# Three Strassen steps in each branch unit, operands laid at any offset, a held preparation, one load moved, and halves, in a hybrid decoder block

## The chip, the cores and the metric

The kernel runs on one core of one Trainium2 chip. The metric is the device time of one execution, in microseconds (us). The profile is of one further execution. In it PE is TensorE's matrix multiplication, PEld its loading of the stationary operand, DVE is VectorE, ACT is ScalarE, POOL is GpSimd, and SP is SyncE, which issues the loads of the weights.

## The reference

One layer of a decoder block on x of 256 rows and 4096 columns, in float32:

```python
h = rmsnorm(x, norm_w)
u_p, z_p, u_c, b_c, c_c, z_c, g_logit = split(h @ w_in)          # 4096 x 20480
y_pool = causal_multiscale_pool(u_p, pool_w, pool_scale) * silu(z_p)
y_conv = causal_gated_shortconv(u_c, b_c, c_c, conv_w, conv_b) * silu(z_c)
br     = [y_pool @ w_branch[0], y_conv @ w_branch[1]]            # 2048 x 4096 each
merged = sum over n of sigmoid(g_logit[n] + gate_b[n]) * br[n]
out    = rmsnorm(x + merged @ w_out, final_norm_w)               # 4096 x 4096
```

## The kernel before

**Products.** Every float32 operand is split into a rounded high part and the remaining low part, and each block product is made of three matmuls: high by high, high by low, low by high. A column of work is a *unit* of 1024 output columns: four for the convolution path twice over (`cz`, `cb`, `cu`, `cc`), two for each half of the pooling path (`pz`, `pu`), eight gate units `g0_0` to `g1_3`, eight branch units `b0_0, b1_0, b0_1, ... b1_3`, and four output units `o0` to `o3`. They run in this order.

**Steps.** A unit is a string of steps, one for each 256 rows of its weight matrix, and the strings at the head of the file (L34 to L48) say which kind each step is. A `P` step is plain: 8 groups of 3 matmuls, 24 in all, into four PSUM banks E (`sums`). An `S` step uses Strassen's scheme with seven block products: 7 groups, 21 matmuls, into three of the banks E and the four banks F (`shared`). The price of an S step is more preparation on the other engines. A branch unit has eight steps.

**Preparation.** A step's weights (1 MB) are loaded by SP into one of three buffers `raw`. For a P step ACT rounds them into four cells of a ring of 15 cells (`highs`), and DVE forms the rest (`lows`). For an S step ACT rounds three cells, DVE forms sums of the quarters in the tile `parts` together with the lows of these three cells (`added`), and then ACT rounds the four sums into four more cells and DVE forms their lows (`split`). `pump` (L964) sends these pieces out in the order of the steps, as far ahead as a limit and free cells allow; it is called after each group of matmuls (`after_group`, L1008), when the cells that this group used have been released. Each engine works through its instructions in the order in which they were sent out.

**Ends of units.** When a bank has had its last matmul, `after_group` at once sends out a copy by ACT: of an E bank into the tile E (or Y), of an F bank into the unit's `join` slot (the tile Y for a gate unit, `last_pair` for a branch unit, E or a `raw` buffer elsewhere). With the last F bank DVE forms the corner sums there, and `combine` (L412) adds them to E. A P step closes its four E banks with its last four groups. An S step at a unit's end takes its products in an order of its own (L340), which closes E with its first three groups; the fourth E bank gets nothing from an S step. What remains to be done for the unit, its epilogue, is a list of items of which one is taken at each *tick*, that is after every 6 matmuls (L998).

**Operands.** The stationary operands (x, then the branches' y, then the merged m) stand in one buffer `arena` of 82 pieces of 1 KB a partition: eight regions of 4 for P, six of 7 and one of 8 for S; a last S region of 8 lies in `last_pair`. `y_ops` (L480) says where the operands of the two branches lie: 6 P and 2 S for branch 0, 5 P and 3 S for branch 1, where one S region of 8 also serves as a P operand in `b1_3`. During `g1_3` and the first branch units these are filled from DRAM through two staging tiles `sa` and `sb`: a load on POOL's queue, eight ticks for landing, then (for S) four sums by DVE, a copy by ACT and the lows by DVE (`Fill`, L751, `pop_fill`, L782). A fill waits until all operands that lay there before have been used. The operands for `o0` are filled in the same way from `b0_3` on.

**The gates.** The epilogue of a gate unit (L671) adds the bias by two accumulating loads on POOL's queue, applies the sigmoid on ACT and stores the result to DRAM (`gates_d`). For the last one, `g1_3`, the gate of branch 0, column 0 is then loaded into Y, on POOL's queue, for `b0_0`'s epilogue, which multiplies with it. The other gates are loaded in the epilogues of the branch units.

Of the kernel before, what the change touches and what calls it, by code (L numbers as in the profile page):

```python
# [15 lines left out]
P = 128  # L16
# [7 lines left out]
KB = 256  # L24
# [18 lines left out]
NINE_B = "PSPSPSPSSPSSPSPS"  # L43
HOST = "PPPBPPMMPSPSSPSSPSS"
OUT3 = "PSPSPSPSPSPSSPPP"
B0 = "PPPPSPSP"
B1 = "PSPSPSPP"
B1_LAST = "PSPPSPPP"  # L48


@with_exitstack
def hybrid_block(ctx: ExitStack, tc: tile.TileContext, x, xc, prm, rows_in, w_in, pool_w, w_branch, w_out, out):
# [101 lines left out]
    def place(region):  # L154
        kind, i = region
        if kind == "p":
            return 4 * KB * i, 4
        if kind == "q":
            return (4 * ND + 14 + 4 * i) * KB, 4
        if i < NS:  # L160
            return (4 * ND + 7 * i) * KB, 7
        return (4 * ND + 7 * NS + 8 * (i - NS)) * KB, 8
# [57 lines left out]
    def highs(cells, src):  # L220
        for i, c in runs(cells):
            act(ring[:, c, 0], src[:, i])
# [14 lines left out]
    class Step:  # L237
        def __init__(self, unit, kind, src=None, op=None, **kw):
            self.unit, self.kind, self.src, self.op = unit, kind, src, op
            self.__dict__.update(kw)  # L240
            self.raw = None
            self.prepared = False
            self.pre, self.mid = [], []

        def first(self):
            if self.kind == "B":
                return []

            def rounded(cells):
                self.q = self.raw.rearrange("p (i c) -> p i c", i=4)  # L250
                self.cells = cells
                if self in steps[:2]:
                    for i in range(4):
                        if self is steps[0] and i == 0:
                            copy(ring[:, cells[0], 0], self.q[:, 0])
                        else:
                            highs(cells[i:i + 1], self.q[:, i:i + 1])
                else:
                    highs(cells, self.q[:, 0:len(cells)])

            return [(3 if self.kind == "S" else 4, None, rounded)]

        def rest(self):
            if self.kind == "P":
                def rests(_):
                    if self in steps[:2]:
                        for i in range(4):
                            if self is steps[0] and i % 2 == 0:
                                x_low(0, 1 - i // 2)
                            lows(self.cells[i:i + 1], self.q[:, i:i + 1])  # L270
                    else:
                        lows(self.cells, self.q)

                return [(None, None, rests)] + self.mid
            if self.kind == "S":
                def added(_):
                    q = self.q
                    add(sums[:, 0:2], q[:, 3:4].to_broadcast([P, 2, NH]), q[:, 1:3])
                    lows(self.cells[2:3], q[:, 2:3])
                    add(sums[:, 2], sums[:, 0], q[:, 2])  # L280
                    lows(self.cells[0:2], q[:, 0:2])
                    add(sums[:, 3], sums[:, 2], q[:, 0])

                def split(cells):
                    self.sum_cells = cells
                    highs(cells[0:2], sums[:, 0:2])
                    for i in (2, 3):
                        highs(cells[i:i + 1], sums[:, i:i + 1])
                    lows(cells[0:2], sums[:, 0:2])
                    lows(cells[2:4], sums[:, 2:4])  # L290

                return [(None, None, added)] + self.mid + [(4, None, split)]
            if self.kind == "B":
                def parts(cells):
                    self.cells = cells
                    highs(cells, quarters(E))
                    lows(cells, quarters(E))

                return [(4, lambda: self.unit.flags.get("base"), parts)]

            def pooled(cells):
                self.pool_cells = cells
                q = quarters(E)[:, 2 * self.g:2 * self.g + 2]
                highs(cells, q)
                lows(cells, q)

            return [(None, None, lambda _: lows(self.cells, self.q)),
                    (2, lambda: self.unit.flags.get(f"pooled{self.g}"), pooled)]
# [160 lines left out]
    def gap(n):  # L469
        return [None] * n  # L470
# [5 lines left out]
    def make_ops(kinds):  # L476
        return [Operand(k, r) for k, r in kinds]

    x_ops = make_ops([("P" if r[0] == "p" else "S", r) for r in x_regions])
    y_ops = [make_ops([("P", ("p", i)) for i in range(6)] + [("S", ("s", i)) for i in (0, 1)]),  # L480
             make_ops([("P", r) for r in (("p", 6), ("p", 7), ("q", 0), ("q", 1), ("q", 2))] +
                      [("S", ("s", i)) for i in (6, 4, 5)])]
    m_ops = make_ops([("P" if r[0] == "p" else "S", r) for r in x_regions])

    def sequence(text, np_, total, both):
# [185 lines left out]
    def gate_unit(n, c):  # L671
        def epi(u):
            def bias(t):
                gather(E[:, t], gate_b[n, None, c * NU:(c + 1) * NU].to_broadcast([P, NU]))

            pause = side_items() + gap(3) if (n, c) == (0, 0) else gap(12)
            return (rescale(E) if u.late else gap(1)) + [lambda: bias(0), lambda: bias(1)] + pause + [
                lambda: act(E[:, 0], E[:, 0], AF.Sigmoid), None,
                lambda: act(E[:, 1], E[:, 1], AF.Sigmoid), lambda: move(gates_d[n, c], E)] + (
                    [lambda: move(Y, gates_d[0, 0])] if (n, c) == (1, 3) else [])  # L680
        text = HOST if (n, c) == (0, 0) else SEVEN3 if (n, c) == (1, 3) else NINE
        u = in_unit(f"g{n}_{c}", 6 * HALF + n * D + c * NU, epi, text)
        u.rotates, u.late = False, (n, c) != (1, 3)
# [4 lines left out]
    def branch_unit(n, c):  # L688
        def epi(u):
            if n == 0:  # L690
                return gap(8) + [lambda: mul(Y, E, Y)]
            turned = spare() if c < 3 else Y

            def gated():
                mul(E, E, spare())
                if c == 3:
                    last_pair["stack"].close()
                    open_last(F32R)
                    last_pair["again"] = True

            def copy(j):
                act(chan(turned)[:, 2 * j:2 * j + 2], bankview(j))

            def stored():
                put(m_d[c], chan(turned))
                merged[c] = now[0] + STORED
            return [lambda: move(spare(), gates_d[1, c])] + gap(6) + [gated, lambda: add(E, E, Y), None,
                lambda: c < 3 and move(Y, gates_d[0, c + 1])] + gap(3) + pairs(transposes(E, copy)) + [stored]

        text = (B1_LAST if c == 3 else B1) if n else B0  # L710
        u = Unit(f"b{n}_{c}", lambda i: w_branch[n, c, i], seq_y(text), y_ops[n], epi)
        u.urgent, u.lead, u.rotates = (lambda: None), 3, False
        units.append(u)
# [104 lines left out]
    insert(names["g0_0"], 1, names["pu1"])  # L818

    steps = [s for u in units for s in u.steps]  # L820
    last = units[-1]
    assert all(s.kind == "P" for s in last.steps[-TAIL:])
    tail = last.steps[-TAIL:]
# [181 lines left out]
            rg.release(part)  # L1005
        state["mm"] += len(mm)

    def after_group(u, b, st):  # L1008
        if u is not last:
            if b in u.total and u.closed([b]) and b not in u.flags:  # L1010
                u.flags[b] = True
                if b[0] == "E":
                    evacuate(u, b[1], b[2])
                else:
                    u.pending.append(b)
        if u.s and u is not last:
            corner_sums(u)
        while state["mm"] >= TICK:
            state["mm"] -= TICK
            tick()  # L1020
        state["limit"] = state["now"] + min(AHEAD, state["now"] + 1)
        if u.urgent and st is u.steps[-1]:
            state["limit"] = state["now"] + u.lead
        pump()

    fetch_x(0)
    act(ssq[:, 0, 0:1], ident[:, 0:1])
    pump()

    def room(o):  # L1030
        return range(o.o, o.o + (4 if o.region[0] in "pq" else 7 if o.region[1] < NS else 8) * KB, KB)

    holders = {c: o for o in x_ops for c in room(o)}
    for ops in (y_ops[0], y_ops[1], m_ops):
# [17 lines left out]
    def run_step(u, st):  # L1052
        if st.kind in "BM":
            (band_sums if st.kind == "B" else mix)(st)
            state["mm"] += 10 if st.kind == "B" else 24
            after_group(u, None, st)
            return
        while not st.op.ready:
            pop_fill(st.op)
        gs = st.groups()  # L1060
        for i, g in enumerate(gs):
            multiply(u, st, g)
            if i == len(gs) - 1:
                st.op.left -= 1
            after_group(u, g[0], st)

    def open_side():
        stack = ExitStack()
# [138 lines left out]
```

## Time and profile before

| | |
|---|---|
| median of 3 runs | 2381.3 us (2380.99 to 2381.68) |
| profiled execution | 2383.08 us, span 2381.4 us |
| granted TensorE clock in it, mean | 0.998 |
| ACT, POOL busy | 63%, 5% |
| data moved | 560.23 MB, 235 GB/s |
| a weight load of 1 MB, median from issue to landing | 4.9 us (w_in), 5.0 us (w_branch, w_out) |

The span runs from the first to the last instruction; the execution's own time is a little longer. A row of the groups or of the timeline gives the line of the code, the engine, the operation, what it writes and reads, its shape and the count, then its time; in square brackets stands how long the engine had been idle before it and what ended that. As nearly every instruction is recorded in a helper, many rows carry the helper's line: L59 is any ACT instruction, L62 a DVE operation on two tensors, L1002 a matmul of a step.

### The profile page before, as it was taken

What the parts mean: (1) busy time and instruction counts of PE and PEld (TensorE: products, weight loads), DVE (VectorE), ACT (ScalarE), POOL (GpSimd) and SP (SyncE); (2) the same over time, 40 slices, a digit from 0 to 9 for tenths busy, and PEclk for the clock granted to TensorE, in tenths of its full rate; (3) what the DMA queues carried; (4) which work ended last, traced back from release to release, by engine and by line L of the source; (5) the groups of instructions that cost most, each with busy time, mean ns of one, the idle gap of its engine ahead of it and who ended that gap; (6) DMA issues with size and microseconds to landing.
All of it is one profiled execution on the core that took longest, in us unless ns stands there. A gap on an engine that the chain in (4) does not pass through costs nothing.

```text
span 2381.4 us, 27763 instructions
## 1 busy us (share of the span) xinstructions
PE 2362.0 (99%) x10481; PEld 1950.3 (82%) x10481; DVE 2153.9 (90%) x2187; ACT 1502.4 (63%) x1626; POOL 113.4 (5%) x173
## 2 busy tenths in 40 slices
PE   9999999999999999999999999999999999999998
PEld 7888888888888888888888888888878888888886
DVE  8889989989989969969999999998998799899998
ACT  6665656666656556656666766666665566566664
POOL 0000000000001000100000000001100000000000
PEclk9999999999999999999999999999999999999999
DMA  9656646656657546746877787778766766767767
GB/s 347 224 196 231 227 171 252 231 204 226 224 180 260 215 176 215 241 176 217 267 250 245 248 249 243 230 255 270 267 252 234 255 231 244 252 210 256 256 218 268
DMA packets 90230, 560.23 MB, mean 235 GB/s; under 512 B 9968, under 2 KB 10224, under 8 KB 29168
## 3 DMA queue, kind: packets, MB, share of 16 engines
q1 hardware_dynamic: 69824, 485.39, 56.4%
q0 software_dynamic: 19696, 71.84, 11.5%
q8 instruction: 82, 1.34, 0.2%
q10 hardware_dynamic: 576, 1.24, 0.1%
q14 instruction: 52, 0.43, 0.1%
HBM read 519.63 MB, written 26.21 MB: 229 GB/s over the span
## 4 chain that ended last, share of the span: by engine, by line
PE 94%; DMA 2%; DVE 2%; ACT 1%; issue 1%; POOL 0%; SPq 0%; DVEq 0%; ACTq 0%; POOLq 0%
PE sums L1002 70%; PE shared L1002 22%; PE shared L656 1%; DMA raw<-in_w_in_dram 1%; PE shared L450 1%; DMA raw<-in_w_branch_dram 1%; ACT ring L59 1%; DVE ring L62 0%; DVE E L62 0%; DVE parts L62 0%; DMA sa<-y_d 0%; DVE raw L62 0%; DVE E L74 0%; ACT E L59 0%; ACT raw L59 0%
## 5 line engine op out<-in xcount | busy, mean ns | idle before, releaser
L1002 PE MATMUL sums<-ring,arena 128*128 128x512 f32 x7305 | 1707.6, 390 | 6.7 <-ACT E L59 3.1
L1002 PEld LDWEIGHTS sums<-ring,arena 128*128 128x128 f32 x7305 | 1371.1, 188 | 294.1 <-ACT E L59 3.5
L62 DVE TENSOR_TENSOR ring<-raw,ring 128x512 fp32r<-128x512 f32 (+3 forms) x720 | 963.2, 1345 | 161.9 <-ACT ring L59 157.1
L59 ACT ACTIVATE ring<-raw 128x1536 fp32r<-128x1536 f32 (+3 forms) x527 | 785.0, 1504 | 282.6 <-PE sums L1002 129.6
L59 ACT ACTIVATE ring<-parts 128x512 fp32r<-128x512 f32 (+1 forms) x621 | 465.6, 763 | 478.7 <-DVE parts L62 409.8
L1002 PE MATMUL shared<-ring,arena 128*128 128x512 f32 x2154 | 518.6, 389 | 0.0
L62 DVE TENSOR_TENSOR ring<-parts,ring 128x1024 fp32r<-128x1024 f32 (+1 forms) x430 | 480.1, 1161 | 7.7 <-ACT ring L59 7.5
L1002 PEld LDWEIGHTS shared<-ring,arena 128*128 128x128 f32 x2154 | 404.3, 188 | 84.1
L62 DVE TENSOR_TENSOR parts<-parts,raw 128x512 f32<-128x512 f32 x406 | 279.4, 688 | 0.0
L62 DVE TENSOR_TENSOR parts<-raw 128x1024 f32<-128x1024 f32 x203 | 247.6, 1220 | 7.7 <-DMA raw<-in_w_in_dram 6.3
L1002 PE MATMUL sums<-ring,last_pair 128*128 128x512 f32 x336 | 84.3, 396 | 0.0
L1002 PEld LDWEIGHTS sums<-ring,last_pair 128*128 128x128 f32 x336 | 63.2, 188 | 15.2
L1002 PE MATMUL shared<-ring,last_pair 128*128 128x512 f32 x192 | 47.6, 397 | 0.0
L59 ACT ACTIVATE E<-sums 128x512 f32<-128x512 f32 x72 | 41.5, 597 | 8.6 <-PE sums L1002 5.2
L1002 PEld LDWEIGHTS shared<-ring,last_pair 128*128 128x128 f32 x192 | 36.1, 188 | 8.7
L62 DVE TENSOR_TENSOR raw<-raw 128x512 f32<-128x512 f32 (+1 forms) x27 | 23.5, 870 | 9.7 <-ACT raw L59 8.8
L59 ACT ACTIVATE E<-sums,rin 128x512 f32<-128x512 f32 x28 | 17.6, 687 | 22.6 <-PE sums L1002 22.6
L62 DVE TENSOR_TENSOR E<-E,last_pair 128x2048 f32<-128x2048 f32 x12 | 27.5, 2289 | 3.3 <-ACT E L59 3.3
L59 ACT ACTIVATE last_pair<-shared 128x512 f32<-128x512 f32 x44 | 24.1, 597 | 9.4 <-PE shared L450 7.7
L62 DVE TENSOR_TENSOR E<-E,Y 128x2048 f32<-128x2048 f32 x13 | 29.7, 2287 | 0.1
L86 POOL DMA_DIRECT2D E<-Y x14 | 16.9, 1449 | 256.1 <-DVE Y L62 200.5
L59 ACT ACTIVATE Y<-shared 128x512 f32<-128x512 f32 x44 | 23.9, 603 | 4.4 <-PE shared L450 4.0
(132 smaller groups left out, 701.2 us busy)
## 6 DMA issues: line engine op xcount, KB each, us to landing
raw<-in_w_in_dram SPq DMA_DIRECT2D x318, 1024.0 KB, 4.9
raw<-in_w_branch_dram SPq DMA_DIRECT2D x64, 1024.0 KB, 5.0
raw<-in_w_out_dram SPq DMA_DIRECT2D x64, 1024.0 KB, 5.0
E<-in_rows_dram POOLq DMA_DIRECT2D x16, 512.0 KB, 6.8
gates_d<-E POOLq DMA_DIRECT2D x8, 1024.0 KB, 6.5
E<-Y POOLq DMA_DIRECT2D x14, 512.0 KB, 8.2
Y<-E POOLq DMA_DIRECT2D x10, 512.0 KB, 8.2
y_d<-E POOLq DMA_DIRECT2D x8, 512.0 KB, 6.7
```

Of the source, the lines that this page charges most:

```text
L59: return pin(nc.scalar.activation(dst, src, func, **kw))
L62: return pin(nc.vector.tensor_tensor(out=dst, in0=a, in1=b, op=op))
L86: return pin(nc.gpsimd.dma_start(dst, src, accum_op=ALU.add))
L450: pin(nc.tensor.transpose(shared(j)[:, i * T + t * P:i * T + (t + 1) * P], src[:, t, c:c + P], ident))
L656: pin(nc.tensor.matmul(o, a, b, start=(k, i) == (0, 0), stop=(k, i) == (3, 2)))
L1002: pin(nc.tensor.matmul(ps, lhs, rhs, start=n == 0, stop=n == u.total[b] - 1))
```

## The change

1. The operands of the branches may lie at any offset of the arena: a region of kind `y` gives its offset and its length. Both branches now have 5 P and 3 S operands, in 41 pieces each.
2. The string of the units `b0_c` becomes `PPPPSSPS` (three S steps in place of two, and an S step at the end), and `b1_3` gets the same string as the other `b1_c`, with three S steps in place of two.
3. During a unit's last step, if it is a P step, `pump` isn't called after the groups 3 to 6.
4. The load of the first gate is moved forward within the epilogue of `g1_3`, from behind the store of its result to the middle of the pause ahead of the sigmoids.
5. A P step that follows an S step is prepared in two halves: `highs` and `lows` each work on two cells at a time in place of four.

```diff
-B0 = "PPPPSPSP"
+B0 = "PPPPSSPS"
 B1 = "PSPSPSPP"
-B1_LAST = "PSPPSPPP"
...
-        if kind == "q":
-            return (4 * ND + 14 + 4 * i) * KB, 4
+        if kind == "y":
+            return i[0] * KB, i[1]
...
+                elif self.halved:
+                    for i in (0, 2):
+                        highs(cells[i:i + 2], self.q[:, i:i + 2])
                 else:
                     highs(cells, self.q[:, 0:len(cells)])
...
+                    elif self.halved:
+                        for i in (0, 2):
+                            lows(self.cells[i:i + 2], self.q[:, i:i + 2])
                     else:
                         lows(self.cells, self.q)
...
-    y_ops = [make_ops([("P", ("p", i)) for i in range(6)] + [("S", ("s", i)) for i in (0, 1)]),
-             make_ops([("P", r) for r in (("p", 6), ("p", 7), ("q", 0), ("q", 1), ("q", 2))] +
-                      [("S", ("s", i)) for i in (6, 4, 5)])]
+    y_ops = [make_ops([("P", ("y", (41 * n + 4 * i, 4))) for i in range(5)] +
+                      [("S", ("y", (i, 7))) for i in ((61, 68, 75) if n else (34, 20, 27))]) for n in range(2)]
...
             pause = side_items() + gap(3) if (n, c) == (0, 0) else gap(12)
+            if (n, c) == (1, 3):
+                pause = gap(5) + [lambda: move(Y, gates_d[0, 0])] + gap(6)
             return (rescale(E) if u.late else gap(1)) + [lambda: bias(0), lambda: bias(1)] + pause + [
                 lambda: act(E[:, 0], E[:, 0], AF.Sigmoid), None,
-                lambda: act(E[:, 1], E[:, 1], AF.Sigmoid), lambda: move(gates_d[n, c], E)] + (
-                    [lambda: move(Y, gates_d[0, 0])] if (n, c) == (1, 3) else [])
+                lambda: act(E[:, 1], E[:, 1], AF.Sigmoid), lambda: move(gates_d[n, c], E)]
...
-        text = (B1_LAST if c == 3 else B1) if n else B0
+        text = B1 if n else B0
...
     steps = [s for u in units for s in u.steps]
+    for a, b in zip(steps, steps[1:]):
+        b.halved = a.kind == "S" and b.kind == "P"
...
-    def after_group(u, b, st):
+    def after_group(u, b, st, hold=False):
...
-        pump()
+        if not hold:
+            pump()
...
-            after_group(u, g[0], st)
+            after_group(u, g[0], st, st is u.steps[-1] and st.kind == "P" and 3 <= i < len(gs) - 1)
```

More of the change, by code (lines that the diff above doesn't have):

```diff
@@ L241, in __init__ @@
             self.raw = None
-            self.prepared = False
+            self.prepared = self.halved = False
             self.pre, self.mid = [], []
@@ L1030, in room @@
     def room(o):
-        return range(o.o, o.o + (4 if o.region[0] in "pq" else 7 if o.region[1] < NS else 8) * KB, KB)
+        return range(o.o, o.o + place(o.region)[1] * KB, KB)
     holders = {c: o for o in x_ops for c in room(o)}
```

## The prediction

> **What bounds the kernel now.** I read the page first, then a piece of the chain of waits, then what PE (TensorE's matmuls) waits for, then the stages that the change touches. Times are us from the span's start.
>
> ```profile
> span 2381.4 us, 27763 instructions
> PE 2362.0 (99%) x10481; PEld 1950.3 (82%) x10481; DVE 2153.9 (90%) x2187; ACT 1502.4 (63%) x1626; POOL 113.4 (5%) x173
> 105.76 7.48 PE sums L1002 x33
> PE sums L1002 <- ACT E L59: 3.1, 1, 3.1
> PE sums L1002 <- ACT Y L59: 2.5, 2, 1.5
> ...
> PE sums L1002 <- DVE ring L743: 0.6, 1, 0.6
> PE sums L1002 <- DVE ring L62: 0.5, 1, 0.5
> ```
>
> PE sets the end: it is busy for 99% of the span. The third row, a piece of the chain of waits, prices a product: 7.48 / 33 = 0.2267 us. The other rows are nearly all that PE waits for: one wait for copies into E, two for copies into Y, and hardly any for DVE. So a gain comes from fewer products, or from these 5.6 us and what follows them; and DVE, at 90%, is close behind. The branch units, by stage:
>
> ```profile
> 1693.30:1738.80 45.50, 42.41 (x188) 34.79 (x187) 39.95 (x45) 29.64 (x34) 5.46 (x9) 1.00 0.83 283
> 1738.80:1782.00 43.20, 43.20 (x184) 35.59 (x185) 42.16 (x38) 27.49 (x29) 0.65 (x2) 0.96 0.58 210
> 1782.00:1825.90 43.90, 43.90 (x203) 36.53 (x202) 34.67 (x30) 24.42 (x28) 3.67 (x6) 1.00 0.75 273
> 1825.90:1867.40 41.50, 41.50 (x184) 34.37 (x184) 38.38 (x29) 25.56 (x25) 0.00 (x0) 1.00 0.60 216
> 1952.90:1996.90 44.00, 44.00 (x204) 36.59 (x203) 38.59 (x37) 27.53 (x36) 5.28 (x9) 1.00 0.79 284
> 1996.90:2039.00 42.10, 42.10 (x187) 34.89 (x186) 40.63 (x43) 27.68 (x30) 2.69 (x5) 1.00 0.67 240
> 1695.80:1770.10 74.30, 71.21 (x307) 58.47 (x307) 70.14 (x74) 45.88 (x51) 6.11 (x10) 0.98 0.70 244
> ```
>
> The rows are units b0_0, b1_0, b0_1, b1_1, b0_3 and b1_3, and a stretch over the first two; after the length stand PE, PEld, DVE, ACT and POOL, then PE's granted clock. In b1_0 DVE is busy for 42.16 of 43.2 us: there it has nothing to spare. In b0_1 it has 9.2 us. This difference decides the forecast.
>
> The one long wait stands between b0_0 and b1_0:
>
> ```profile
> 1722.16 10.68 DMA raw<-in_w_branch_dram
> 1729.39 6.28 PE L1002 MATMUL sums<-ring,arena 128*128 128x512 f32 x27
> 1732.86 1.22 DVE L62 TENSOR_TENSOR parts<-raw 128x1024 f32<-128x1024 f32 x1 [1.44 <-DMA raw<-in_w_branch_dram]
> 1737.59 0.63 ACT L59 ACTIVATE ring<-parts 128x512 fp32r<-128x512 f32 x1 [0.26 <-DVE parts L62]
> 1738.13 2.04 ACT L59 ACTIVATE E<-sums 128x512 f32<-128x512 f32 x4
> 1738.76 8.69 PE L1002 MATMUL sums<-ring,arena 128*128 128x512 f32 x30 [3.09 <-ACT E L59]
> 1747.29 2.88 PE L1002 MATMUL shared<-ring,arena 128*128 128x512 f32 x12
> ```
>
> A weight load needed 10.68 us, against a median of 5.0. DVE began that S step at 1732.86, ACT made its last sums at 1737.59, and only behind them, in program order, came the four copies out of the banks that b1_0's first P step overwrites. PE should have gone on at 1729.39 + 27 x 0.2267 = 1735.51 and did at 1738.76: 3.25 us. Its next 30 products took 1747.29 - 1738.76 = 8.53 us instead of 6.80, at half rate in part: 1.73 more. Price of this place: 5.0 us.
>
> **The change, part by part.** *Five P steps become S steps* (one in each b0_c, one in b1_3). A P step has 24 products, an S step 21: 5 x 3 x 0.2267 = **-3.4 us** of PE.
>
> *The wait at the end of b0_0.* b0_c now ends in S, whose closing order shuts three E banks in the first 9 of 21 products and the fourth one step earlier. The copies so have 12 products, 2.7 us, and more before b1_c's first step needs the banks, where now the last one has none. The g units end in S too, and PE's list above has no wait for E but this one. I take the whole **-5.0 us** (bounds: 0, were the copies again behind late sums, and -5.0).
>
> *The moved load.* Y <- gates_d (1 MB on POOL's queue) goes nine ticks behind g1_3's combination instead of behind the sigmoids:
>
> ```profile
> 1703.74 0.87 POOL L86 DMA_DIRECT2D E<-in_rows_dram  x1 [0.32 <-issue]
> 1710.37 0.57 POOL L83 DMA_DIRECT2D sa<-y_d  x1 [5.76 <-DVE sb L62]
> 1714.71 0.56 POOL L83 DMA_DIRECT2D sb<-y_d  x1 [3.77 <-DVE arena L62]
> 1721.39 0.53 POOL L83 DMA_DIRECT2D Y<-gates_d  x1
> ```
>
> It passes two fills' loads and the gates' store, and should issue just behind the load at 1710.37 (the fills of the sixth to eighth tick are in front of it), 10 us sooner. It needs Y free (its last reader is the combination, before 1703.74). The weight load of 1722.16 loses a competitor; those of the ten us before gain one. No queue waits longer than a few us; its own worth is inside the -5.0.
>
> *No preparation between a unit's last closings.* I find nothing that it removes. The ring has 15 cells, a P takes 4, an S 3 and then 4. At a last P with PS behind it 4 + 4 + 7 = 15 are taken, and the next P needs all four cells of the running one, the last of which comes free with group 7, which isn't held. With P behind it, the one preparation that fits goes out at group 1, before the hold begins at 3. So the two waits for Y (2.5 us, behind cz1 and pz0) stay, apart from what the halves shorten: **-0.2 us** (bounds 0 and -3).
>
> *Halves.* Every P behind an S (172 such pairs now) is prepared in two ACT and two DVE instructions in place of one each. Durations on DVE are read from start to start:
>
> ```profile
> 1737.99 2.67 DVE L62 TENSOR_TENSOR last_pair<-last_pair 128x512 f32<-128x512 f32 x3
> 1740.58 2.35 DVE L62 TENSOR_TENSOR ring<-parts,ring 128x1024 fp32r<-128x1024 f32 x2
> 1742.85 2.29 DVE L62 TENSOR_TENSOR ring<-raw,ring 128x2048 fp32r<-128x2048 f32 x1
> 1745.05 2.28 DVE L62 TENSOR_TENSOR E<-E,last_pair 128x2048 f32<-128x2048 f32 x1
> 1747.26 1.22 DVE L62 TENSOR_TENSOR parts<-raw 128x1024 f32<-128x1024 f32 x1
> 1751.34 1.01 DVE L62 TENSOR_TENSOR sb<-sb 128x128 f32<-128x128 f32 x4
> 1752.26 2.35 DVE L62 TENSOR_TENSOR ring<-parts,ring 128x1024 fp32r<-128x1024 f32 x2
> 1754.54 0.69 DVE L62 TENSOR_TENSOR arena<-sa,arena 128x512 fp32r<-128x512 f32 x1
> 1755.14 2.28 DVE L62 TENSOR_TENSOR ring<-raw,ring 128x2048 fp32r<-128x2048 f32 x1
> 1767.79 2.29 DVE L62 TENSOR_TENSOR ring<-raw,ring 128x2048 fp32r<-128x2048 f32 x1 [0.75 <-ACT ring L59]
> 1770.41 29.86 PE L1002 MATMUL sums<-ring,arena 128*128 128x512 f32 x131
> ```
>
> The lows of a P: 1745.05 - 1742.85 = 2.20. Two of 1024: 1754.54 - 1752.26 = 2.28, so halving costs 0.08 each, and PE may begin 1.14 earlier. An S: 1754.54 - 1747.26, less 0.92 of a fill's sums in it, = 6.36. Corner sums 2.59, the combination 2.21, a P fill 0.60.
>
> [...]
>
> *What five S steps cost DVE.* 6.36 - 2.20 = 4.16 each. In b0_0 and b1_0 there is no room. The last row of the stage table has DVE busy for 70.14 us from 1695.8 (where it had waited for weights) to 1770.1, the end of the lows of b1_0's seventh step, a P. That step began at 1770.41 + 3 x 0.2267 = 1771.09: one us to spare, *after* the old wait had given DVE 5.0. Without the wait and with three products fewer PE wants it at 1693.3 + (183 + 135) x 0.2267 = 1765.4. DVE needs 70.14 + 4.16 + 5 x 0.08 - 1.14 (only the first half is wanted at once) = 73.6, without a pause: 1769.4. It is **late by 3.8 at least**, by 8.0 if its 4.16 us of pauses stay. Laid out step by step with the durations above, the corner sums now behind b0_0's last step, DVE meets b1_0's fourth step 2.6 us late and its sixth 1.6: I take **+4.2 us** (3.8 is nearest, since most pauses were for the late load). So the wait taken from one end is mostly paid at the other.
>
> In b0_1 and b0_2 the second S fits into DVE's 9.2 us, and b1_1 has 41.5 - 38.38 = 3.1 us besides: 0. In b0_3 and b1_3 the fills for o0 come on top. b1_3's DVE work becomes 40.63 + 4.16 + 0.3 = 45.1 in 41.4, most of it early. From the lows of its first P (about 1991.1 by the ring's cells) to the first lows that its sixth step, an S, needs, I count 33.4 us: two S, two P, corner sums, the combination, the gate product, the fills, and 3.5 of that S. That is 2024.5; PE comes at 1996.9 - 0.7 + 114 x 0.2267 = 2022.0, and at its second product 0.2 later: **+2.3 us** (0 to 4).
>
> The other fills: y0 has an S fill (1.9) for a P fill (0.6), done during g1_3, and by a count of ticks every fill is ready within four ticks of where it is now, at least two steps before its use. Cost 0; if one were late, its four sums, copy and lows would stand before PE, about 3 us.
>
> Sum: -3.4 - 5.0 - 0.2 + 4.2 + 2.3 = **-2.1 us**. The profiled execution took 2383.1 for a span of 2381.4, and the median of the runs is 2381.3, so I set the sum against both alike: span 2379.3, median **2379.2**.
>
> **Rivals.** *All of it is kept*: DVE's pauses shrink and the halves cover the rest: -8.6, 2372.7. For it: PE's waits for DVE are near nothing today. Against it: 42.16 of 43.2. *And the held preparation works too*, -2.8 more: 2369.9. For it: both waits for Y stand at a last P. Against it: the count of cells.
>
> *The new wait falls in one piece* of over 3 us, and PE runs at half rate behind it, 1.7 as now: 2380.9. The waits of 1.5 us at most, for Y, were followed by no half rate. [...]
>
> *Slower*: the second S of a pair needs seven cells where the P had four. If they aren't free in time, DVE can't use its pauses in b0_c, and each b1_c gets 4.16 + 0.3 + 2.6 (corner sums one step later) - 1.1 = 6.0 against 3.1 spare: 2.9 late in each of four pairs, 11.6 on top: 2390.8. It decides whether DVE starts the second S before PE starts the first. For it: S, S takes 14 of 15 cells. Against it: the g units have SS without a wait.
>
> **How the numbers follow.** Forecast 0.45; all kept 0.25; the hold too 0.05; half rate 0.13; slower 0.12. The likeliest's own range, from its bounds, is 2376.5 (3.8 and 0) to 2384.7 (8.0 and 4). 2371.8 to 2385.0 takes in all but the hold's case, the slower one and a little more. 0.2% is 4.8 us, about what can be told from no change: faster (below 2376.5) 0.30 and 0.04 of the forecast's low end, 0.34; slower (above 2386.1) 0.12; within, 0.54.
>
> **What would show it.** No wait for E between b0_0 and b1_0 and no half rate at 1740; Y <- gates_d near 1711; 15 products fewer; PE waiting for DVE's ring in b1_0's fourth and sixth step, some 4 us, and in b1_3; the waits for Y behind cz1 and pz0 still there. I am wrong if b1_0 runs without a wait (all kept), or if b1_1 and b1_2 show waits too (slower).

## The result, and the profile after

| | before | after |
|---|---|---|
| median of 20 runs each, same chip | 2380.87 us (2379.06 to 2383.09) | 2386.21 us (2383.75 to 2388.87) |
| profiled execution, its span | 2383.08, 2381.4 us | 2387.33, 2385.6 us |

The ratio of after to before is 1.0022, with a 95% interval of 1.0015 to 1.0029: the change made the kernel 5.3 us slower, where 2.1 us faster was forecast, and 2386.2 lies outside the forecast's range, which ended at 2385.0.

The page of the changed kernel, and what PE waits for in it (us in total, times, longest):

```profile
span 2385.6 us, 28246 instructions
PE 2360.6 (99%) x10466; PEld 1946.0 (82%) x10466; DVE 2184.3 (92%) x2389; ACT 1523.5 (64%) x1810; POOL 113.0 (5%) x173
...
PE sums L1009 <- DVE ring L61: 6.8, 5, 1.8
PE sums L1009 <- ACT E L58: 3.0, 1, 3.0
```

PE has the 15 products fewer that were meant (10481 to 10466). But waits for DVE's ring cells, 0.5 us before, are now 6.8 us: one of 1.8 in the first 20 us of the kernel, in spite of which the branches begin earlier than before, and 5.0 in b0_0 and b1_0. And there is one wait for copies into E again, of 3.0 us, at another place than before. The stages, in the columns of the prediction: length, PE, PEld, DVE, ACT, POOL, PE's granted clock, DMA share, GB/s. The rows are b0_0, b1_0, then b0_3, b1_3, o0, a stretch over b0_0 and b1_0, and then the two middle pairs, b0_1 with b1_1 and b0_2 with b1_2:

```profile
1692.20:1736.50 44.30, 42.16 (x185) 34.15 (x184) 39.56 (x48) 28.58 (x35) 5.04 (x8) 1.00 0.79 263
1736.50:1782.70 46.20, 43.01 (x184) 33.67 (x182) 46.03 (x50) 30.06 (x39) 1.61 (x3) 1.00 0.60 220
1952.40:1995.70 43.30, 43.30 (x200) 36.00 (x199) 40.44 (x42) 28.07 (x38) 5.28 (x9) 1.00 0.79 277
1995.70:2041.40 45.70, 42.25 (x184) 34.01 (x182) 45.32 (x53) 29.94 (x37) 2.69 (x5) 1.00 0.60 219
2041.40:2128.30 86.90, 86.89 (x383) 71.54 (x384) 79.24 (x94) 51.65 (x60) 4.73 (x8) 0.98 0.63 223
1695.40:1782.70 87.30, 81.98 (x353) 65.17 (x351) 85.39 (x96) 55.44 (x70) 6.65 (x11) 1.00 0.70 243
...
1782.70:1867.60 84.90, 84.90 (x383) 70.46 (x383) 79.48 (x72) 53.00 (x64) 3.67 (x6) 1.00 0.68 248
1867.60:1952.40 84.80, 84.80 (x383) 70.35 (x382) 77.28 (x70) 52.33 (x63) 2.56 (x4) 1.00 0.66 238
```

Of o0 the kernel before has this row:

```profile
2039.00:2124.00 85.00, 85.00 (x383) 70.36 (x382) 76.69 (x87) 50.87 (x54) 4.74 (x8) 1.00 0.63 221
```

Read pair by pair against the prediction's table. The middle pairs have PE busy from end to end, and each is shorter by about the 0.68 us of its three products (the pair of b0_1 was 43.9 + 41.5 = 85.4 and is 84.9). The first pair went from 45.5 + 43.2 = 88.7 to 44.3 + 46.2 = 90.5. It has 366 products, 83.0 us at 0.2267: it now loses 7.5 us, in the pair where DVE is busy for 85.39 of 87.3 us. At the other end b1_3 grew from 42.1 to 45.7 and o0 from 85.0 to 86.9; with three products fewer that is 3.6 + 1.9 + 0.7 = 6.2 us lost. The branches begin 1.1 us earlier (1693.3 to 1692.2), and from o1 to the end the length is the same within 0.1 us. The whole: -1.1 + 1.8 - 0.5 - 0.7 - 0.7 + 3.6 + 1.9 = +4.3, against 4.2 between the spans.

The first place, as PE sees it (start, length, engine and line, what it writes and reads, count; in brackets the idle time before and what ended it):

```profile
1724.68 7.11 PE L1009 MATMUL sums<-ring,arena 128*128 128x512 f32 x30 [0.76 <-DVE ring L61]
1733.17 0.73 PE L1009 MATMUL sums<-ring,arena 128*128 128x512 f32 x2 [1.38 <-DVE ring L61]
...
1754.00 1.45 PE L1009 MATMUL sums<-ring,arena 128*128 128x512 f32 x5 [1.32 <-DVE ring L61]
...
1766.82 1.42 PE L1009 MATMUL sums<-ring,arena 128*128 128x512 f32 x5 [1.55 <-DVE ring L61]
```

The first two rows are in b0_0's seventh step, a P, and in its last, an S; the others are in b1_0's fourth and sixth, both S. No wait is long; PE stops where it needs cells that DVE hasn't filled. These four and one of 0.3 us are 5.3 of the 7.5 us; the rest is spread over the products around the stops. Why DVE is late already in b0_0 shows in ACT's rows there, and in one of DVE's:

```profile
1717.90 0.63 ACT L58 ACTIVATE arena<-sa 128x512 fp32r<-128x512 f32 x1 [4.83 <-DMA sa<-y_d]
1718.44 2.09 ACT L58 ACTIVATE ring<-parts 128x1024 fp32r<-128x1024 f32 x3
1720.43 1.99 ACT L58 ACTIVATE E<-E 128x1024 f32<-128x1024 f32 x2
1722.33 1.99 ACT L58 ACTIVATE ring<-raw 128x1024 fp32r<-128x1024 f32 x2
```

```profile
1723.40 2.36 DVE L61 TENSOR_TENSOR ring<-raw,ring 128x1024 fp32r<-128x1024 f32 x2 [1.51 <-ACT ring L58]
```

ACT took its work in the order of these rows. It stood 4.83 us for a fill's load; the S step's copies, two sigmoids and then the next copies followed without a gap, and DVE, which needed the last of these, lost 1.51 us. It is most of what DVE was idle in the 87.3 us (1.9). Up to the end of the first half of the lows for b1_0's seventh step, the stretch that the prediction reckoned, the changed kernel has this row:

```profile
1695.40:1771.30 75.90, 70.58 (x303) 55.97 (x302) 74.06 (x86) 45.64 (x60) 6.65 (x11) 1.00 0.68 233
```

The second place, the end of b1_3, on ACT and then on PE:

```profile
2033.28 1.92 ACT L58 ACTIVATE ring<-raw 128x2048 fp32r<-128x2048 f32 x1 [1.05 <-DMA raw<-in_w_out_dram]
2035.21 0.64 ACT L58 ACTIVATE arena<-sb 128x512 fp32r<-128x512 f32 x1
2037.78 2.00 ACT L58 ACTIVATE ring<-raw 128x1024 fp32r<-128x1024 f32 x2 [1.93 <-PE sums L1009]
2039.93 0.95 ACT L58 ACTIVATE arena<-sa 128x896 fp32r<-128x896 f32 x1
2040.78 2.04 ACT L58 ACTIVATE E<-sums 128x512 f32<-128x512 f32 x4
```

```profile
2041.41 7.80 PE L1009 MATMUL sums<-ring,arena 128*128 128x512 f32 x26 [3.00 <-ACT E L58]
```

and the same place in the kernel before:

```profile
2033.40 0.63 ACT L59 ACTIVATE arena<-sb 128x512 fp32r<-128x512 f32 x1 [1.78 <-DMA sb<-m_d]
2033.94 0.94 ACT L59 ACTIVATE arena<-sa 128x896 fp32r<-128x896 f32 x1
2034.79 1.99 ACT L59 ACTIVATE ring<-raw 128x1024 fp32r<-128x1024 f32 x2
2037.19 2.64 ACT L59 ACTIVATE E<-sums 128x512 f32<-128x512 f32 x4 [0.41 <-PE sums L1002]
```

Before, the copies for the next step (`ring<-raw`) and the fill's copy (`arena<-sa`) were done by 2037, and ACT stood ready for the four copies out of the banks. After, both came behind 2037, and the four copies behind them: 2040.78. That is the old wait between b0_0 and b1_0 over again, with 3.0 us, and with half rate behind it: PE's granted clock was 0.50 from 2042 to 2044 us and 1.00 again from 2045, and 26 products took 7.80 us, where 5.9 are the full rate (26 x 0.2267). The row of 2037.78 gives PE as the releaser; but the weights that it copies, issued at 2031.99, took 5.7 us to land, to 2037.7, so the row alone doesn't say which of the two held it. A kernel of the experiments with the same order of work there (the one without the combination in the middle units) shows the weights in that row:

```profile
2036.14 2.00 ACT L58 ACTIVATE ring<-raw 128x1024 fp32r<-128x1024 f32 x2 [1.93 <-DMA raw<-in_w_out_dram]
```

And the load went out late behind DVE. In the changed kernel SP issues it when DVE ends the first of two `lows` out of a `raw` buffer, near 2031.9:

```profile
2029.68 4.49 DVE L61 TENSOR_TENSOR ring<-raw,ring 128x2048 fp32r<-128x2048 f32 x2
2031.99 0.33 SPq L76 DMA_DIRECT2D raw<-in_w_out_dram  x1
```

That is 6.4 us ahead of the time at which b1_3's last product ended; in the kernel before the load for this copy was issued at 2026.27, 12.7 us ahead.

### The profile page after: what moved, and what is told of

Same layout as the page of the kernel before. It is cut to its first block, busy times and chain, and to the rows that moved or that the text cites. A ratio compares the mean times of both kernels' runs of the same rounds, so it can differ in the third digit from the quotient of the medians.

```text
span 2385.6 us, 28246 instructions
## 1 busy us (share of the span) xinstructions
PE 2360.6 (99%) x10466; PEld 1946.0 (82%) x10466; DVE 2184.3 (92%) x2389; ACT 1523.5 (64%) x1810; POOL 113.0 (5%) x173
## 5 line engine op out<-in xcount | busy, mean ns | idle before, releaser
L1009 PE MATMUL sums<-ring,arena 128*128 128x512 f32 x7230 | 1693.3, 390 | 11.7 <-DVE ring L61 6.8
L1009 PEld LDWEIGHTS sums<-ring,arena 128*128 128x128 f32 x7230 | 1356.1, 188 | 298.3 <-DVE ring L61 9.7
L61 DVE TENSOR_TENSOR ring<-raw,ring 128x1024 fp32r<-128x1024 f32 (+2 forms) x892 | 972.2, 1110 | 128.3 <-ACT ring L58 125.9
L58 ACT ACTIVATE ring<-raw 128x1024 fp32r<-128x1024 f32 (+3 forms) x696 | 800.9, 1183 | 306.1 <-PE sums L1009 108.9
L58 ACT ACTIVATE ring<-parts 128x512 fp32r<-128x512 f32 (+1 forms) x636 | 473.6, 762 | 439.0 <-DVE parts L61 374.3
L1009 PE MATMUL shared<-ring,arena 128*128 128x512 f32 x2214 | 534.0, 389 | 0.7 <-DVE ring L61 0.6
L61 DVE TENSOR_TENSOR ring<-parts,ring 128x1024 fp32r<-128x1024 f32 (+1 forms) x441 | 491.7, 1158 | 18.1 <-ACT ring L58 18.1
L1009 PEld LDWEIGHTS shared<-ring,arena 128*128 128x128 f32 x2214 | 415.3, 188 | 88.3 <-DVE ring L61 1.9
L61 DVE TENSOR_TENSOR parts<-parts,raw 128x512 f32<-128x512 f32 x416 | 285.6, 686 | 0.0
L61 DVE TENSOR_TENSOR parts<-raw 128x1024 f32<-128x1024 f32 x208 | 253.6, 1219 | 5.3 <-DMA raw<-in_w_in_dram 5.3
L58 ACT ACTIVATE E<-sums 128x512 f32<-128x512 f32 x72 | 41.5, 595 | 9.6 <-PE sums L1009 6.4
```

Source lines behind the costliest of these rows:

```text
L58: return pin(nc.scalar.activation(dst, src, func, **kw))
L61: return pin(nc.vector.tensor_tensor(out=dst, in0=a, in1=b, op=op))
L1009: pin(nc.tensor.matmul(ps, lhs, rhs, start=n == 0, stop=n == u.total[b] - 1))
```

## The experiments

Each run is told by its median and its ratio to runs of the kernel before on the same chip.

**Is it DVE's work in the first and the last pair?** The combination (2.2 us of DVE) is left out of b0_0 and b0_3, so that their corner sums aren't added; in a second kernel it is left out of b0_1 and b0_2 instead.

```diff
-            else:
+            elif u.name not in ("b0_0", "b0_3"):
                 add(d4, d4, q)
```

> The changed kernel without the DVE addition of the corner sums to E in b0_0 and b0_3 (2.2 us of DVE work each, left out). Theory (DVE is late in b0_0/b1_0, 7.5 us of waits, and at the end of b1_3, 6.0 with half rate): 2.2 us come back in b1_0 and 2.2 or more at the end of b1_3, so 2378 to 2382 against 2386.2. Rival (the waits come from late weight loads, or from the ring's cells): no change, 2386.

> The same addition left out in b0_1 and b0_2, where the profile shows no wait. Theory (DVE work costs only where DVE has nothing to spare): no change, 2386. Rival (every branch unit that ends in S pays): as much as without the additions of b0_0 and b0_3, some 4 us.

Without it in the outer units: 2382.16 us, 1.0001 (0.9992 to 1.0010). In the middle units: 2386.45 us, 1.0021 (1.0013 to 1.0030), as the changed kernel. By the medians the same two instructions are worth 4 us at one place and nothing at the other. The row of b1_0 in the first kernel, then in the second:

```profile
1734.30:1778.30 44.00, 42.44 (x184) 33.78 (x182) 43.83 (x49) 30.10 (x39) 1.61 (x3) 1.00 0.63 231
```

```profile
1734.40:1780.70 46.30, 43.11 (x185) 33.74 (x183) 46.13 (x50) 30.13 (x39) 1.61 (x3) 1.00 0.60 220
```

b1_0 gives back 46.2 - 44.0 = 2.2 us, the whole duration of the instruction: with DVE busy for 46.03 of 46.20 us in the changed kernel, DVE is the bound there, not PE. At the other end nothing came back in this execution: PE's wait for E ahead of o0 was 3.7 us. Where the rest of the 4 us lies in the other executions, one profile doesn't show; the two profiled executions themselves are 1.9 us apart (2383.43 and 2385.37).

**One of the five S steps alone.** The kernel before, with the third S step in b1_3.

```diff
-        text = (B1_LAST if c == 3 else B1) if n else B0
+        text = B1 if n else B0
```

> The kernel before with one edit, b1_3 with three S steps in place of two. Theory (the third S of b1_3 makes DVE late beside the fills for o0): the wait between b1_3 and o0 appears, though smaller since b0_3 still has two S: +1 to +5 against before, 2382 to 2386. Rival (the wait there comes from b0_3's third S or from its ending in S): 0.7 us of products saved and no wait, 2380.2.

2383.20 us, 1.0008 (0.9999 to 1.0016): 2.0 us slower by the medians, not settled by the interval. The waits are elsewhere than in the changed kernel: b1_3 stayed at 42.3 us and o0 took 86.2, with PE waiting 1.4 us for DVE ahead of transposes, 1.0 of it in o0. So in b1_3 the third S step isn't enough to make the late copies. In the changed kernel, where b0_3 ahead of it has a third one too and ends in S, they are late; which of these two does it, no run separates.

**The halves**, taken out of the changed kernel.

```diff
-        b.halved = a.kind == "S" and b.kind == "P"
+        b.halved = False
```

> The changed kernel with every P prepared in one piece again. Theory (halving costs DVE 0.08 us a step, but PE may begin 1.1 us earlier at a P behind an S): the waits at b1_0's P steps grow, +1 to +3, 2387 to 2389. Rival (172 more instructions on DVE and ACT are what makes DVE late): -2 to -5, 2381 to 2384.

2389.26 us, 1.0031 (1.0019 to 1.0043): 3 us more by the medians than with them, 2 by the ratios, and the two intervals overlap. In its profile the first pair takes 46.1 + 46.5 = 92.6 us, against 90.5. Of these 2.1 us 1.8 are in b0_0, where 20 products take 6.42 us in place of 4.5:

```profile
1726.82 6.42 PE L1009 MATMUL sums<-ring,arena 128*128 128x512 f32 x20 [1.82 <-DVE ring L61]
```

So what the halves earn in this pair is mainly the half rate that doesn't come: without them PE stands 0.64 and then 1.82 us at the step at which it stood 0.76 with them, and its mean granted clock over b0_0 is 0.96 in place of 1.00.

**Can the hold mend the end of b1_3?** The hold as it stands covers the groups 3 to 6. Without it the instruction streams of the changed kernel are the same on all five engines, so it does nothing, as forecast; it was not run. Here it begins at group 0:

```diff
-            after_group(u, g[0], st, st is u.steps[-1] and st.kind == "P" and 3 <= i < len(gs) - 1)
+            after_group(u, g[0], st, st is u.steps[-1] and st.kind == "P" and i < len(gs) - 1)
```

> The changed kernel with the preparation held from the first group of a unit's last P step, not from its fourth: the rounding of a later P's weights, which ACT sends out at group 1 ahead of the copies out of E, now stands behind them. Theory (at the end of b1_3 ACT stands still for a late weight load with the copies out of E behind it, 3.2 us and half rate after it): that wait goes, -3 to -5, 2381 to 2383. Rival (DVE's lateness alone makes the wait, in whatever order): no change, 2386.

2387.36 us, 1.0027 (1.0016 to 1.0038): nothing gained. ACT at the end of b1_3:

```profile
2039.35 0.95 ACT L58 ACTIVATE arena<-sa 128x896 fp32r<-128x896 f32 x1 [3.94 <-DVE sa L61]
2040.21 2.04 ACT L58 ACTIVATE E<-sums 128x512 f32<-128x512 f32 x4
2042.12 2.02 ACT L58 ACTIVATE ring<-raw 128x1024 fp32r<-128x1024 f32 x2
```

The copies for the next step now stand behind those out of E, as wanted. But the fill's copy still stands ahead of them and waits 3.94 us for its sums on DVE. So there were two things in the way, either of them enough. The next kernel also holds the fills back until the copies out of E are sent out:

```diff
+        closing[0] = hold
...
-            if f.at is not None and f.free() and (now[0] >= f.at + LANDING or f.o is force):
+            if not closing[0] and f.at is not None and f.free() and (now[0] >= f.at + LANDING or f.o is force):
```

> The changed kernel with the preparation held from the first group of a unit's last P step and, beside it, no fill moved on until the copies out of E have been sent out. Theory (at the end of b1_3 the copies out of E stand on ACT behind a fill's copy, which waits for sums that DVE makes late): the wait of 3.0 us and the half rate behind it go, -3 to -5, 2381 to 2383. Rival (DVE's lateness would show at b1_3's next P anyway): a wait for DVE's ring in its place, 2385 to 2387.

```profile
PE sums L1010 <- DVE ring L61: 7.3, 6, 1.8
PE shared L455 <- DVE E L61: 3.7, 5, 2.1
```

The wait for E is gone from the list, which shows that the order on ACT made it. The time is the same as the changed kernel's: 2386.38 us, 1.0022 (1.0013 to 1.0031). In its place stand waits for DVE, for ring cells (7.3, from 6.8) and for E ahead of transposes (3.7, of which the longest, 2.1, is in o0). With the load that waited for DVE's `lows`, that speaks for DVE's lateness behind both, and for the order on ACT as what chose where PE felt it. It is not shown by relief: the kernel without b0_3's combination has the wait for E all the same (3.7 us).

**Relief for DVE: the fills' sums and lows on POOL**, which is busy for 5%.

```diff
+    def ptt(dst, a, b, op):
+        return pin(nc.gpsimd.tensor_tensor(out=dst, in0=a, in1=b, op=op))
...
-                sums_s(self.st)
+                psums(self.st)
...
-                sub(o.view[:, 1], q, o.view[:, 0].bitcast(F32))
+                ptt(o.view[:, 1], q, o.view[:, 0].bitcast(F32), ALU.subtract)
```

> The changed kernel with the fills' sums and lows (8.7 us of DVE work for the 8 fills of b1, 5 to 7 for those of o0 in b1_3) done by POOL. Theory (DVE has too much work in b0_0/b1_0 and b1_3): the waits of 7.5 and 6.0 us go for the most part, -8 to -13, 2373 to 2378. Rival (POOL is so slow, or so much in DVE's way, that fills are late): no change or slower.

2402.66 us, 1.0092 (1.0078 to 1.0105): 16 us worse than the changed kernel. Of this kernel the costliest group on POOL (busy and mean ns), then a stretch of b0_0 on DVE and on POOL:

```profile
L742 POOL TENSOR_TENSOR arena<-sa,arena 128x512 fp32r<-128x512 f32 (+2 forms) x15 | 40.9, 2725 | 46.2 <-ACT arena L58 46.1
```

```profile
1715.23 2.63 DVE L61 TENSOR_TENSOR ring<-raw,ring 128x512 fp32r<-128x512 f32 x1
1717.78 2.25 DVE L61 TENSOR_TENSOR parts<-parts,raw 128x512 f32<-128x512 f32 x1
```

```profile
1714.93 2.37 POOL L742 TENSOR_TENSOR arena<-sb,arena 128x896 fp32r<-128x896 f32 x1 [3.07 <-ACT arena L58]
...
1718.19 1.27 POOL L742 TENSOR_TENSOR arena<-sa,arena 128x512 fp32r<-128x512 f32 x1
```

In the changed kernel the same two operations are:

```profile
1714.99 0.69 DVE L61 TENSOR_TENSOR ring<-raw,ring 128x512 fp32r<-128x512 f32 x1
1715.59 0.68 DVE L61 TENSOR_TENSOR parts<-parts,raw 128x512 f32<-128x512 f32 x1
```

Beside POOL's they took 2.63 and 2.25 us in place of 0.69 and 0.68. DVE's busy time rose from 2184.3 to 2204.1 us though it had 88 instructions fewer. In this form it is no relief. How the 16 us divide between DVE's longer instructions and fills that POOL brings late, the runs don't show.

**The load of the first gate**, put back behind the sigmoids' store in the changed kernel.

```diff
-                pause = gap(5) + [lambda: move(Y, gates_d[0, 0])] + gap(6)
...
+                    [lambda: move(Y, gates_d[0, 0])] if (n, c) == (1, 3) else [])
```

> The changed kernel with the load of the first gate back behind the sigmoids. Theory (in b0_0 and b1_0 DVE's work sets the pace, not the weights): -0.5 to +1. Rival A (the moved load delays a fill's load and with it ACT, which makes the first wait in b0_0): -1 to -2. Rival B (the old place makes the weights late for b1_0 again): +2 to +5.

2385.88 us, 1.0022 (1.0014 to 1.0031): no difference from the changed kernel. The waits in b0_0 are there as before (0.64 and 1.39 us), so it isn't the moved load that makes them. Ahead of b1_0 its profile has a short wait for copies out of E, 0.5 us; with S at b0_0's end there is little that a late weight load could lengthen. Ahead of o0 it has 5.0 us in place of 3.0, in an execution of 2388.07 us; whether the load has to do with that, one profile doesn't show.

**The change without its S steps**: the kernel before with the halves and the moved load, and its own strings and operands. A second kernel has the halves without the moved load.

```diff
+    for a, b in zip(steps, steps[1:]):
+        b.halved = a.kind == "S" and b.kind == "P"
...
+            if (n, c) == (1, 3):
+                pause = gap(5) + [lambda: move(Y, gates_d[0, 0])] + gap(6)
```

> The kernel before with the moved load and the halves, and its old strings and operands. Theory (without its wait of 5.0 us DVE would be 3 to 4 us late in b1_0 all the same): -1 to -3 against before, 2378 to 2380. Rival (the 5.0 us were the late weights alone): -5 or more, 2376.

> The kernel before with the halves alone: its old strings of steps, its old operands and the load of the first gate at its old place; against the version with halves and the moved load, which took 2377.0. Theory 1 (the halves carry the gain: without them the changed kernel was 3 us slower, and with the load put back it was the same): 2377 to 2378.5, both waits for Y gone, the wait for copies into E between b0_0 and b1_0 still 1.7 to 3.3 us. Theory 2 (in the old order of steps the load at its old place competes with the late weight load of b1_0, so that the move earns its part there): 2379 to 2381, with a wait for E of over 3 us and products at half rate behind it.

With both: **2377.01 us** (2376.27 to 2378.45), 0.9984 (0.9975 to 0.9993): faster than both kernels, 3.9 us under before and 9.2 under after. With the halves alone: 2379.73 us (2378.37 to 2383.12), 0.9996 (0.9987 to 1.0005), on another chip; the intervals overlap a little, but the traces have the difference at one place. PE at the start of b1_0, with the halves alone and then with both:

```profile
1735.15 8.73 PE L1010 MATMUL sums<-ring,arena 128*128 128x512 f32 x30 [2.67 <-ACT E L59]
```

```profile
1735.04 7.14 PE L1011 MATMUL sums<-ring,arena 128*128 128x512 f32 x30 [1.70 <-ACT E L59]
```

The wait is shorter by 1.0 us, and the half rate behind it (8.73 - 7.14 = 1.6 us in 30 products) is gone: 2.6 together. Each against the kernel before on its own chip, the medians have gains of 3.9 and 2.0 us, 1.9 apart; the ratios are 0.0012 apart, 2.9 us. So in the old order of steps the moved load earns its part, as theory 2 had it, about 2 to 3 us, and the halves about 1 to 2. The load's path is seen on POOL's queue, where `Y<-gates_d` went out at 1718.35 with the halves alone, ahead of the late weight load, and at 1708.59 with both; ACT's wait for these weights went from 3.79 to 1.07 us.

**Ending in S by itself**: the version of 2377.0 with b0_c = `PPPPSPPS`, with two S steps as before, one of them last.

```diff
-B0 = "PPPPSPSP"
+B0 = "PPPPSPPS"
```

> The kernel before with the moved load, the halves and the string PPPPSPPS for b0: two S steps as before, but an S at the end. Theory (ending in S takes the copies out of E off the path, and it is the third S that makes DVE late): the 1.9 us that are left between b0_0 and b1_0 go, 2375 to 2376, against 2377.0 with the old string. Rival (the late corner sums of a unit that ends in S cost DVE as much in b1_0): 2377 to 2379.

```profile
PE sums L1011 <- DVE ring L62: 3.0, 3, 2.0
PE shared L456 <- DVE E L62: 1.5, 3, 1.1
```

2380.69 us, 0.9999 (0.9990 to 1.0008): 3.7 us more than with P at the end, with the same number of products. The wait for E is gone, and waits for DVE stand in its place: 2.9 us in b1_0's fourth and sixth step and 1.1 ahead of transposes in o0. It fits that with S last the corner sums and the combination come in b1_c's first steps, where DVE has no room, while with P last a whole step of PE covers them; no run moves that work alone.

**The kernel before once more**, to see how much of the old waits one execution shows.

> The kernel before, profiled once more. Theory (the waits for Y behind cz1 and pz0 are there in every execution, and the halves take them away): 1.1 and 1.7 us again. Rival (they were an accident of one execution): no such waits, and the halves are worth less than 1 us ahead of the branch units.

```profile
PE sums L1002 <- ACT E L59: 2.5, 1, 2.5
...
PE sums L1002 <- ACT Y L59: 0.9, 1, 0.9
```

2380.74 us, a single run. The wait for E is there with 2.5 us, the waits for Y only once, with 0.9. All four profiles without halves have a wait for Y (0.9 to 2.5 us in all), and none of the ten with halves has one. The branches begin at 1691.6 to 1693.3 us without halves and, with them, at 1690.0 to 1691.0 in nine executions; the profiled one of the changed kernel, with 1692.2, had lost some 1.6 us to half rate in its first 25 us (last section).

Between these versions stands the account of the change, by medians (of runs on different chips, so to about 1 us): halves and moved load -3.9; S at the end of b0_c +3.7; five S steps in place of P steps, with the new operands, 2386.2 - 2380.7 = +5.5, of which -3.4 is their 15 products and some +8.9 are waits and half rate.

## Why the prediction failed

*Products*, -3.4: right, shown by the count and by the two middle pairs, which are shorter by about that (0.5 and 0.7 us for 0.68) and have no wait.

*The second S in b0_1 and b0_2 at no cost*: right. b1_1 and b1_2 run without a wait, and leaving out DVE work there changed nothing. The slower rival (late ring cells in all four pairs) didn't happen; the kernel came out slower by another way.

*The old wait*, -5.0: it went as forecast, and the load went out at 1711.79, as forecast. But ending in S by itself, with the halves and the moved load, left the time where it was (0.9999), and 3.7 us above the same kernel with P last: what the wait had cost came back as waits for DVE. The sentence "So the wait taken from one end is mostly paid at the other" said so.

*b0_0 and b1_0*, +4.2: the mechanism was right and the size was not; it measured 7.5, inside the bounds of 3.8 to 8.0. The step that failed is "3.8 is nearest, since most pauses were for the late load". It supposed that DVE runs without a pause from 1695.8, so that b0_0 itself has no wait. PE waits 0.76 and 1.38 us in b0_0, behind a DVE that ACT's copies, late behind a fill's load, had held up. The waits in b1_0 stand in the fourth and sixth step, as laid out. The prediction's own sum accounts for the size: its two times, 1769.4 and 1765.4, are 4.0 apart, not 3.8, and the row of 1695.40 adds 1.8 us of pauses, 0.5 of work (74.1 for 73.6), and a start 0.8 later after b0_0's first product (3.2 for 2.5 us). That is 7.1 of the 7.5.

*b1_3*, +2.3 (0 to 4): the step counted DVE's work up to b1_3's sixth step, and there little is lost: one wait of 0.3 us, and 1.2 us in the whole unit beside the wait at its end. This is the second step that failed: it took DVE's lateness to reach PE only through the ring's cells, and left out the end of the unit. b1_3 ends in a P step, as the old b0_0 did, whose late copies out of E had just been priced; weights that were late behind DVE and a fill's copy make the same wait there. It cost 3.0 us, and the half rate behind it 1.9 more (o0's 86.9 against 85.0). The mechanism and its price were in the prediction, but for b0_0; they weren't asked of the other unit that ends in P. The runs with the longer hold show that moving ACT's order takes this wait away and puts DVE's in its place.

*Halves*, -0.2 (0 to -3): too small. The term stood for the two waits for Y, which were forecast to stay; no profile with halves has one, and the kernel before shows 2.5 us of them in one execution and 0.9 in another, so part of the 2.5 was that one execution's. Taken out of the changed kernel the halves are worth 2 to 3 us, in the order of before about 1 to 2. The 0.08 us that one costs was the smaller side.

*The hold*, nothing: right, and shown for a longer one. *The moved load*, "its own worth is inside the -5.0": right for the changed kernel, where it is nothing. In the old order it is 2 to 3, which no term had asked.

By terms, the misses are 7.5 - 4.2 = +3.3 in the first pair, 6.2 - 2.3 = +3.9 in b1_3 and o0, and -1.1 + 0.2 = -0.9 ahead of the branches; -2.1 + 6.3 = +4.2, the difference of the spans. The rival of the half rate was true in kind and stood at o0, not in b1_0. The -0.9 holds for the profiled execution: others with halves begin the branches 1 to 2 us earlier.

## What to carry to other kernels

Where a second engine is busy for 98% of a stage (here DVE for 85.39 of 87.3 us), price every addition there at its full duration, and leave none of its gaps as a cushion; the same step was free in the middle pairs and cost more than its gain in the outer ones. When a wait is found at one unit's end, list every unit that ends the same way and ask what would make it late too. Ask where a wait that is taken away would come back while an engine lags (here the 3.0 us for E came back as 0.5 more for ring cells and 3.3 more ahead of transposes): take the cheap parts alone (here the halves and the moved load, 3.9 us faster) before those that add work to the lagging engine.

## What the hardware showed that was not expected

*DVE's operations took longer beside POOL's.* One operation on two tensors, 128x512, took 2.63 us on DVE while POOL worked on one of its own (2.37 us, begun 0.30 earlier), and 0.69 in the changed kernel, without POOL's: a factor of 3.8.

*Half rate came behind shorter waits than supposed, and the length of the wait alone didn't decide it.* The prediction's rival had it behind one wait of over 3 us. In the kernel before it is behind 3.09 us: PE's granted clock was 1.00 until 1739.8, 0.50 from 1740.3 to 1743.0 and 1.00 again from 1744.0. In the changed kernel it is behind the 3.00 us ahead of o0. The two kernels without a combination wait 3.7 and 3.2 us there, and o0's mean clock is 0.97 and 0.98, against 1.00 in the kernel before. Behind 2.67 us (halves alone), 2.54 (the kernel before once more) and 2.39 the same 30 products at the start of b1_0 took 8.73, 8.68 and 8.70 us. The last of these is in the kernel before with a third S step in b1_3:

```profile
1736.78 8.70 PE L1002 MATMUL sums<-ring,arena 128*128 128x512 f32 x30 [2.39 <-ACT E L59]
```

With the halves and the moved load, behind 1.70 us, these 30 products took 7.14 us. There was no half rate either behind 2.04 us in b1_0 with S at b0_0's end (5 products in 1.43 us, and in 1.45 behind 1.32 us in the changed kernel), or behind 2.12 us ahead of transposes with the longer hold and the fills held (8 transposes in 1.09 us, as behind 0.26). But without halves in the changed kernel 1.82 us, with another of 0.64 just ahead of it, was enough: 20 products in 6.42 us in place of 4.5. The plainest pair is the wait in the first 20 us, in the changed kernel and in the one without the combination in b0_0 and b0_3:

```profile
19.60 5.07 PE L1009 MATMUL sums<-ring,arena 128*128 128x512 f32 x14 [1.83 <-DVE ring L61]
```

```profile
19.32 3.45 PE L1009 MATMUL sums<-ring,arena 128*128 128x512 f32 x14 [1.83 <-DVE ring L61]
```

Behind the same 1.83 us the granted clock was 0.50 from 21.0 to 24.0 us in the first, and its 14 products took 5.07 us; the second's took 3.45. So between 1.8 and 2.1 us it went either way here, and what decides there isn't shown. In the old order with the halves, the moved load made a wait 1.0 us shorter (2.67 to 1.70) and gained 2.6, with the 1.6 of half rate behind it.
